# Gate rows of a gated DeltaNet layer read back from HBM, a mask for two heads at once, and one logarithm for queries and keys

## The chip, the cores and the metric

The kernel runs on one core of a Trainium2 chip. The metric is the device time of one execution in microseconds (us); smaller is better. Three runs of the kernel before gave 2562.58, 2562.96 and 2564.0 us, a median of 2562.96 us.

A core has five engines that run side by side, each working through its own queue in order: PE (TensorE, matrix products; its weight loads are listed as PEld), DVE (VectorE, elementwise work), ACT (ScalarE, functions and copies), POOL (GpSimd) and SP (SyncE, which here issues the transfers between HBM and the on-chip memory). An engine waits in its queue until what its next instruction needs is there.

## The reference

The reference is a trunk of two layers over 256 tokens of width 2048, in float32:

```python
for i in range(DEPTH):                       # DEPTH = 2
    h = rms_norm(x, mixer_norm[i])
    x = x + (diff_attention(h, ...) if i % 2 == 0 else gated_deltanet(h, ...))
    x = x + conv_ffn(rms_norm(x, ffn_norm[i]), ...)
```

The change lies in the gated DeltaNet mixer of layer 1. It has 16 heads of queries and keys and 32 value heads, so each query/key head serves two value heads. What matters here of its reference:

```python
q = l2_norm(q.reshape(b, s, 16, 128)); k = l2_norm(k.reshape(b, s, 16, 128))
beta = sigmoid(b_gate)
g = -exp(a_log) * softplus(a_gate + dt_bias)
# per value head and per chunk of 64 tokens
q = q * 128 ** -0.5
g_c = cumsum(g)
decay = exp(where(tril, g_c[:, None] - g_c[None, :], -inf))
low = where(strict, (k * beta) @ k.T * decay, 0)
qk  = where(tril, q @ k.T * decay, 0)
```

The kernel works with two blocks of 128 tokens in place of chunks of 64. For each value head it needs the decay of every token against every other one: the exponential of a running sum along a row, plus a column term per token (the negative running sum and the logarithm of beta), with the later tokens masked out. The running sum of a head is one row of 256 numbers; to stand in the decay table, which has 128 partitions, it must be present in all of them.

## The kernel before, in words

Weights stream from HBM through the core. `weights` (lines 72 to 85) loads a chunk of 512 KB into the tile `raw` (3 buffers, issued by SP, L82), ACT copies it rounded into `whi` (4 buffers, L83), and DVE subtracts to get the rest, `wlo` (4 buffers, L84). `dense` (L95) multiplies a chunk into PSUM: in the DeltaNet layer three products per weight tile (L110, L111, L113); `dense_tok` (L140) does the same with tokens on the partitions (L153 to L155). After every chunk the generators in `bg` advance by one step (`tick`, L67); each `yield` in them puts what follows one chunk later in program order. The framework then writes each engine's queue: it takes instructions in program order as priority, lets one go ahead when its own estimate says that its inputs and a buffer are there, and fills gaps with later ones. The order on an engine is fixed from then on.

`gdn` (L439) runs the mixer. First comes the gate projection, from which `gates` (L732) makes `col` (a column term per token and head, L775) and `rows` (the running sums of all 32 heads as rows, L777 to L782; the rounded value in partitions 0 to 31 and the rest in 32 to 63). Then four blocks of four query/key heads follow. In a block the order of chunks is: the four query/key projections, one value projection, two groups of the output gate `z` (dense_tok), the other value projections; and then, from the second block on, the output projection of the block before (`out`, L687).

For each query/key head `keys` (L485) runs as a generator:

- It squares queries and keys (`sq`, L488), and splits the squares into two parts (`sp`, L489).
- For each of the two value heads POOL spreads a column of the constant `hot` into a 128 x 128 selector (L500), and PE multiplies the selector with `rows` (L502), which puts that head's row into all partitions of a PSUM bank. DVE adds column term and mask, in two instructions per value head (L505), into `d`. 
- PE sums the squares over the partitions (`total`, L241). ACT takes two logarithms, one for the queries and one for the keys (L511 and L512), because the queries' carries the factor 128, then one exponential for both (L513). 
- ACT takes two exponentials per value head (L516 and L517), the second straight from PSUM.
- PE multiplies keys with keys and queries with keys (L525, L526), and DVE multiplies these with `d` into `lt` and `qkt` (L531, L532). POOL copies blocks of `lt` into `Cc` (L536).

`invert` (L540) and `levels` (L565) invert the triangular matrices, and `group` (L618) makes the outputs of two query/key heads; its last step transposes them (L679) for the output projection.

Of the kernel before, what the change touches and what calls it, by code (L numbers as in the profile page):

```python
# [8 lines left out]
F32 = mybir.dt.float32  # L9
# [7 lines left out]
P = 128  # L17
# [8 lines left out]
class Trunk:  # L26
# [8 lines left out]
    def __init__(self, ctx, tc):  # L35
# [402 lines left out]

    def gdn(self, w_gate, w_in, w_z, w_out, nb, hb, gate_ap, const_ap, hot_ap, conv_col, ng, done):  # L439

# [11 lines left out]
        with tc.tile_pool(name="gd", bufs=1) as gd:  # L452
            self.spawn(self.norm_stat())
            con = gd.tile([P, 384], F32, tag="con", name="con")[:, :384]
            nc.sync.dma_start(con, const_ap)
            ident, mask, triu = con[:, :P], con[:, P:T], con[:, T:]
            hot = gd.tile([P, nv], F32, tag="hot", name="hot")
            nc.sync.dma_start(hot, hot_ap)
            gp = gd.tile([P, 2, nv], F32, tag="gp", name="gp")
            nc.sync.dma_start(gp, gate_ap)  # L460
            eps128 = gd.tile([P, 1], F32, tag="eps128", name="eps128")
            nc.vector.memset(eps128, P * EPS)
            TTs, Tas = [], []
# [21 lines left out]
            def keys(hq, c, cc, b0, res):  # L485

                sq = gd.tile([P, 2, T], F32, tag="qs", name="qs", bufs=2)
                nc.scalar.square(sq, c)  # L488
                sp = gd.tile([P, 2, 2, T], F32R, tag="qp", name="qp", bufs=1)  # L489
                self.split(sp, sq)  # L490
                yield
                yield
                while "rows" not in gates:
                    yield
                gb, gc = mp(), gates["col"]
                ds = []
                for v in range(2):
                    h = 2 * hq + v
                    sel = gd.tile([P, P], F32R, tag="sel", name="sel", bufs=2)
                    nc.gpsimd.tensor_copy(sel, hot[:, h:h + 1].to_broadcast([P, P]))  # L500
                    g = gb[:, v * T:(v + 1) * T]
                    nc.tensor.matmul(g, sel, gates["rows"], start=True, stop=True)  # L502
                    d = gd.tile([P, 384], F32, tag="d", name="d", bufs=2)
                    for t in range(2):
                        nc.vector.scalar_tensor_tensor(  # L505
                            d[:, (1 - t) * P:(2 - t) * P], g[:, t * P:(t + 1) * P], gc[:, t, h:h + 1], mask, ALU.add, ALU.add)
                    ds.append(d)
                pn = mp()
                with self.lnexp(self.total(pn, [sp])):
                    pq, pk = self.apart(pn)[:, 0, :], self.apart(pn)[:, 1, :]  # L510
                    nc.scalar.activation(sq[:, 0, :], pq, AF.Ln, bias=eps128, scale=float(P))  # L511
                    nc.scalar.activation(sq[:, 1, :], pk, AF.Ln, bias=self.eps, scale=1.0)  # L512
                    nc.scalar.activation(sq, sq, AF.Exp, scale=-0.5)  # L513
                    for v, d in enumerate(ds):
                        h = 2 * hq + v
                        nc.scalar.activation(d[:, :T], d[:, :T], AF.Exp)  # L516
                        nc.scalar.activation(d[:, T:], gb[:, v * T + P:(v + 1) * T], AF.Exp, bias=gc[:, 0, h:h + 1])  # L517
                nc.vector.tensor_tensor(c, c, sq, ALU.mult)
                q, k = c[:, 0, :], c[:, 1, :]
                yield  # L520
                yield
                prods = []
                for r in (k, q):
                    p = mp()
                    nc.tensor.matmul(p[:, :P], k[:, P:], r[:, P:], start=True, stop=True)  # L525
                    nc.tensor.matmul(p[:, P:384], k[:, :P], r, start=True, stop=True)  # L526
                    prods.append(p)
                for v in range(2):
                    lt = gd.tile([P, 384], F32, tag="lt", name="lt", bufs=2 * hb)
                    qkt = gd.tile([P, 384], F32, tag="qkt", name="qkt", bufs=2 * hb)  # L530
                    nc.vector.tensor_tensor(lt, prods[0][:, :384], ds[v], ALU.mult)  # L531
                    nc.vector.tensor_tensor(qkt, prods[1][:, :384], ds[v], ALU.mult)  # L532
                    b = b0 + v
                    lv = lt[:, :T].rearrange("p (t c) -> p t c", t=2)
# [3 lines left out]
                    res.append((lt, qkt))  # L538

# [78 lines left out]
            def group(gi, gr, lqs, inv, vt, ready, zts, acts):  # L618
# [73 lines left out]
            pg = self.dense(w_gate, KD, self.h_acts, tiles=1, wide=False)  # L692
            self.spawn(self.gates(gd, pg, nv, gp, ident, triu, gates))
            pend = None
# [36 lines left out]

    def gates(self, gd, pg, nv, gp, ident, triu, res):  # L732

        nc, mp = self.nc, self.mp
        t0 = gd.tile([P, 4, 2, 64], F32, tag="vz", name="gt0", bufs=4)
        t1 = gd.tile([P, 4, 2, 64], F32, tag="vz", name="gt1", bufs=4)
# [42 lines left out]
        nc.tensor.matmul(pr[:, P:], w[:, 1, :], triu, start=False, stop=True)  # L779
        rows = gd.tile([P, T], F32R, tag="grow", name="grow")  # L780
        nc.scalar.copy(rows, pr)
# [16 lines left out]
def _layout(inputs):  # L798
# [41 lines left out]
    def turned(w):  # L840
# [18 lines left out]
        "const": np.concatenate(const, 1).astype(f),  # L859
        "hot": np.concatenate([np.eye(NV)] * 2 + [np.zeros((P - 2 * NV, NV))]).astype(f),  # L860
        "w_up1": blocks(x["ffn_w_up"][1], KD, up),
# [5 lines left out]
def trunk_kernel(tc, a, out):  # L867
    nc = tc.nc
    with ExitStack() as ctx:
# [30 lines left out]
        def start(k):  # L900

            if len(begun) <= k:
# [11 lines left out]
        t.ffn(a["w_up0"], a["w_down0"], NJ, a["fcols0"], then(mixer, 1))  # L914
        t.gdn(a["w_gate"], a["w_in"], a["w_z"], a["w_out"], NB, HB, a["gate"], a["const"], a["hot"],
              lambda tap, tile_: one(gconv, tap * 4 * NQ + tile_), ng, then(ffn, 1))
# [17 lines left out]
```

## Time and profile before

| what | value |
|---|---|
| median of three runs | 2562.96 us |
| the profiled execution | 2563.51 us |
| its span, first to last instruction | 2561.7 us |
| mean granted clock of TensorE | 0.998 |
| PE busy | 2541.3 us |
| DVE busy | 1910.1 us |
| ACT busy | 1503.9 us |
| POOL busy | 107.1 us |
| DeltaNet mixer | about 1063 to 1885 us of the span |

The profiled execution is 0.55 us above the median, and 1.8 us of it lie outside the span. "Busy" of PE counts a product from its start to its modelled end; products are pipelined, so that one may start about 0.11 us after another and still be listed with 0.28 us. What a product costs is read from the distance between starts.

### The profile page before, as it was taken

Reading aid. Unit: us, or ns where it says so; the run is one execution under the profiler, and the core shown is the slowest. Engines: PE = TensorE matmul, PEld = TensorE weight load, DVE = VectorE, ACT = ScalarE, POOL = GpSimd, SP = SyncE. Lnnn points to the kernel's source line nnn. Section 1 sums busy time; section 2 is a strip of 40 time slices with the busy share of each in tenths; the row PEclk is TensorE's granted clock in tenths of the full one; section 3 lists DMA queues with packets and bytes.
Section 4 is the critical chain, followed back from the end, with each engine's and each line's share of the span. In section 5 each row is a group of like instructions: output and inputs, shape, how many; then the busy total and the mean of one; then the engine's idle time right before and its main releaser. Section 6 shows DMA issues by size and latency. Waiting matters only on the chain.

```text
span 2561.7 us, 44240 instructions
## 1 busy us (share of the span) xinstructions
PE 2541.3 (99%) x17456; PEld 2366.3 (92%) x17456; DVE 1910.1 (75%) x2846; ACT 1503.9 (59%) x2094; POOL 107.1 (4%) x221
## 2 busy tenths in 40 slices
PE   8999999999999999999999999999999999999999
PEld 7998899999999999999989999999999999999998
DVE  7876677777878655689789688689687778786554
ACT  6666656666666444585674674674566666665433
POOL 0000000000000000010121021021000000000000
PEclk9999999999999999999999999999999999999999
DMA  6555566665666666656455455455466666666665
GB/s 216 184 178 174 173 199 202 202 201 202 201 201 203 199 203 200 193 166 198 141 161 194 133 177 182 138 167 188 148 200 201 202 201 202 200 200 207 207 209 162
DMA packets 135425, 481.02 MB, mean 188 GB/s; under 512 B 15409, under 2 KB 18481, under 8 KB 135217
## 3 DMA queue, kind: packets, MB, share of 16 engines
q1 hardware_dynamic: 134064, 475.58, 57.8%
q8 instruction: 137, 2.24, 0.3%
q10 hardware_dynamic: 1152, 2.61, 0.3%
q14 instruction: 72, 0.58, 0.1%
HBM read 476.03 MB, written 2.10 MB: 187 GB/s over the span
## 4 chain that ended last, share of the span: by engine, by line
PE 94%; DVE 2%; ACT 2%; issue 1%; DMA 1%; POOL 0%; SPq 0%; ACTq 0%; DVEq 0%
PE ps L110 47%; PE ps L111 27%; PE ps L113 6%; PE ps L153 3%; PE ps L154 3%; PE ps L155 3%; PE mp L635 2%; DVE wlo L84 1%; PE mp L241 1%; ACT whi L83 1%; DMA raw<-w_in 0%; PE mp L526 0%; PE mp L605 0%; PE mp L600 0%; DMA raw<-w_qk 0%
## 5 line engine op out<-in xcount | busy, mean ns | idle before, releaser
L84 DVE TENSOR_TENSOR wlo<-raw,whi 128x1024 fp32r<-128x1024 f32 (+2 forms) x909 | 1104.5, 1216 | 546.9 <-ACT whi L83 538.7
L83 ACT CAST whi<-raw 128x1024 fp32r<-128x1024 f32 (+2 forms) x909 | 944.4, 1040 | 853.7 <-PE ps L110 597.3
L110 PE MATMUL ps<-h,whi 128*128 128x512 f32 (+1 forms) x4304 | 1363.4, 358 | 9.6 <-DVE h L168 6.0
L111 PE MATMUL ps<-h,wlo 128*128 128x256 f32 x4304 | 1181.0, 274 | 1.5 <-DVE wlo L84 1.5
L110 PEld LDWEIGHTS ps<-h,whi 128*128 128x128 f32 x4304 | 818.9, 190 | 96.8 <-DVE h L168 6.0
L111 PEld LDWEIGHTS ps<-h,wlo 128*128 128x128 f32 x4304 | 828.5, 193 | 3.6 <-DVE wlo L84 2.3
L110 PE MATMUL ps<-ac,whi 128*128 128x512 f32 x1632 | 535.0, 382 | 0.0
L111 PE MATMUL ps<-ac,wlo 128*128 128x256 f32 x1632 | 444.7, 273 | 0.0
L110 PEld LDWEIGHTS ps<-ac,whi 128*128 128x128 f32 x1632 | 308.4, 189 | 42.9 <-PE ps L110 0.2
L111 PEld LDWEIGHTS ps<-ac,wlo 128*128 128x128 f32 x1632 | 313.3, 192 | 0.1
L113 PE MATMUL ps<-h,whi 128*128 128x256 f32 x1040 | 287.3, 276 | 0.0
L113 PEld LDWEIGHTS ps<-h,whi 128*128 128x128 f32 x1040 | 200.3, 193 | 0.4
L154 PE MATMUL ps<-wlo,h 128*128 128x512 f32 x384 | 146.2, 381 | 0.0
L155 PE MATMUL ps<-whi,h 128*128 128x512 f32 x384 | 145.9, 380 | 0.0
L153 PE MATMUL ps<-whi,h 128*128 128x512 f32 x384 | 145.8, 380 | 0.0
L222 DVE SCALAR_TENSOR_TENSOR cv<-u,fcols,cv 128x255 f32<-128x255 f32 (+1 forms) x344 | 142.8, 477 | 0.0
L111 PE MATMUL ps<-oc,wlo 128*128 128x256 f32 x512 | 141.9, 277 | 0.0
L110 PE MATMUL ps<-oc,whi 128*128 128x256 f32 x512 | 141.7, 277 | 0.0
L113 PE MATMUL ps<-oc,whi 128*128 128x256 f32 x512 | 141.4, 277 | 0.0
L111 PEld LDWEIGHTS ps<-oc,wlo 128*128 128x128 f32 x512 | 98.3, 192 | 0.2
L110 PEld LDWEIGHTS ps<-oc,whi 128*128 128x128 f32 x512 | 98.3, 192 | 0.2
L113 PEld LDWEIGHTS ps<-oc,whi 128*128 128x128 f32 x512 | 98.2, 192 | 0.1
(201 smaller groups left out, 2108.5 us busy)
## 6 DMA issues: line engine op xcount, KB each, us to landing
raw<-w_up SPq DMA_DIRECT2D x344, 512.0 KB, 4.7
raw<-w_down SPq DMA_DIRECT2D x160, 512.0 KB, 3.7
raw<-w_in SPq DMA_DIRECT2D x128, 512.0 KB, 4.5
raw<-w_z SPq DMA_DIRECT2D x64, 512.0 KB, 3.6
raw<-w_out SPq DMA_DIRECT2D x64, 512.0 KB, 4.4
raw<-w_qk SPq DMA_DIRECT2D x63, 512.0 KB, 4.5
raw<-w_v SPq DMA_DIRECT2D x32, 512.0 KB, 3.5
raw<-w_o SPq DMA_DIRECT2D x32, 512.0 KB, 4.5
```

The lines of the kernel that those rows point to most:

```text
L83: nc.scalar.copy(hi, raw)
L84: nc.vector.tensor_tensor(lo, raw, hi.bitcast(F32), ALU.subtract)
L110: nc.tensor.matmul(ps[:, c, :n], hi[:, k, s], self.turns(a[:, :n // T, :]), start=first, stop=False)
L111: nc.tensor.matmul(ps[:, c, :T], lo[:, k, s], self.turns(a[:, :1, :]), start=False, stop=last and wide)
L113: nc.tensor.matmul(ps[:, c, :T], hi[:, k, s], self.turns(a[:, 1:, :]), start=False, stop=last)
L153: nc.tensor.matmul(ps[:, c, :], ah, wh, start=first, stop=False)
L154: nc.tensor.matmul(ps[:, c, :], ah, wl, start=False, stop=False)
L155: nc.tensor.matmul(ps[:, c, :], al, wh, start=False, stop=last)
L222: nc.vector.scalar_tensor_tensor(out[:, j:], u[:, :T - j], taps[n - 1 - j], out[:, j:], ALU.mult, ALU.add)
L241: last = self.nc.tensor.matmul(out, self.onesr, self.pairs(p[:, j]), start=i + j == 0, stop=i + j == n)
L635: nc.tensor.matmul(p[:, v, :], l(v), r[:, v, :], start=i == 0, stop=i == len(terms) - 1)
```

## The change

The running sums of the 32 heads are laid out as 32 rows of 384 numbers: the second block of 128 tokens, then both blocks. They are written to a buffer in HBM once. For each query/key head a transfer then reads two rows of it (one for each value head) and puts them into all 128 partitions of a tile `d` of 128 x 2 x 384. That takes the place of the selectors, the selector products and the constant `hot`. The mask is added to both value heads in one DVE instruction; the column term moves into the bias of the exponentials. One logarithm serves queries and keys, and the queries' factor moves into the product that makes `qkt`. The tiles `lt`, `qkt` and `d` hold both value heads; `d` has still two buffers, so that it now holds two query/key heads. The triangle `triu` and the rows before their transfer lie in a buffer of the tag `qs`, which the squares use too. The second set of rows in partitions 32 to 63 is gone. `group` yields once more ahead of its transposes.

```diff
+        self.dr = ctx.enter_context(tc.tile_pool(name="dr", bufs=1, space=bass.MemoryType.DRAM))
...
-            con = gd.tile([P, 384], F32, tag="con", name="con")[:, :384]
-            nc.sync.dma_start(con, const_ap)
-            ident, mask, triu = con[:, :P], con[:, P:T], con[:, T:]
-            hot = gd.tile([P, nv], F32, tag="hot", name="hot")
-            nc.sync.dma_start(hot, hot_ap)
+            con = gd.tile([P, T], F32, tag="con", name="con")
+            nc.sync.dma_start(con, const_ap[:, :T])
+            ident, mask = con[:, :P], con[:, P:]
+            early = gd.tile([P, 2 * T], F32, tag="qs", name="early", bufs=2)
+            nc.sync.dma_start(early[:, :P], const_ap[:, T:])
...
-                gb, gc = mp(), gates["col"]
-                ds = []
-                for v in range(2):
-                    h = 2 * hq + v
-                    sel = gd.tile([P, P], F32R, tag="sel", name="sel", bufs=2)
-                    nc.gpsimd.tensor_copy(sel, hot[:, h:h + 1].to_broadcast([P, P]))
-                    g = gb[:, v * T:(v + 1) * T]
-                    nc.tensor.matmul(g, sel, gates["rows"], start=True, stop=True)
-                    d = gd.tile([P, 384], F32, tag="d", name="d", bufs=2)
-                    for t in range(2):
-                        nc.vector.scalar_tensor_tensor(
-                            d[:, (1 - t) * P:(2 - t) * P], g[:, t * P:(t + 1) * P], gc[:, t, h:h + 1], mask, ALU.add, ALU.add)
-                    ds.append(d)
+                gc = gates["col"]
+                d = gd.tile([P, 2, 384], F32, tag="d", name="d", bufs=2)
+                nc.sync.dma_start(d, gates["rows"][2 * hq:2 * hq + 2, :].unsqueeze(0).to_broadcast([P, 2, 384]))
+                dv = d[:, :, :T].rearrange("p v (t c) -> p v t c", t=2)
+                m4 = mask.unsqueeze(1).unsqueeze(1).to_broadcast([P, 2, 2, P])
+                nc.vector.tensor_tensor(dv, dv, m4, ALU.add)
                 pn = mp()
                 with self.lnexp(self.total(pn, [sp])):
-                    pq, pk = self.apart(pn)[:, 0, :], self.apart(pn)[:, 1, :]
-                    nc.scalar.activation(sq[:, 0, :], pq, AF.Ln, bias=eps128, scale=float(P))
-                    nc.scalar.activation(sq[:, 1, :], pk, AF.Ln, bias=self.eps, scale=1.0)
-                    nc.scalar.activation(sq, sq, AF.Exp, scale=-0.5)
-                    for v, d in enumerate(ds):
-                        h = 2 * hq + v
-                        nc.scalar.activation(d[:, :T], d[:, :T], AF.Exp)
-                        nc.scalar.activation(d[:, T:], gb[:, v * T + P:(v + 1) * T], AF.Exp, bias=gc[:, 0, h:h + 1])
+                    self.rsqrt(sq, self.apart(pn), 1)
+                    for v in range(2):
+                        for t, s in ((1, d[:, v, :P]), (0, d[:, v, P:])):
+                            nc.scalar.activation(s, s, AF.Exp, bias=gc[:, t, 2 * hq + v:2 * hq + v + 1])
...
+                lt = gd.tile([P, 2, 384], F32, tag="lt", name="lt", bufs=hb)
+                qkt = gd.tile([P, 2, 384], F32, tag="qkt", name="qkt", bufs=hb)
                 for v in range(2):
-                    lt = gd.tile([P, 384], F32, tag="lt", name="lt", bufs=2 * hb)
-                    qkt = gd.tile([P, 384], F32, tag="qkt", name="qkt", bufs=2 * hb)
-                    nc.vector.tensor_tensor(lt, prods[0][:, :384], ds[v], ALU.mult)
-                    nc.vector.tensor_tensor(qkt, prods[1][:, :384], ds[v], ALU.mult)
+                    nc.vector.tensor_tensor(lt[:, v], prods[0][:, :384], d[:, v], ALU.mult)
+                    nc.vector.scalar_tensor_tensor(
+                        qkt[:, v], prods[1][:, :384], P ** -0.5, d[:, v], ALU.mult, ALU.mult)
+                for v in range(2):
...
                     ys.append(y)
                 yield
                 yield
+                yield
                 for v0 in range(0, n, 2):
...
-            for d in range(2):
-                nc.vector.scalar_tensor_tensor(
-                    w[:, t, 32 * d:32 * d + nv], q[:, t, nv:], -1.0, a, ALU.mult, ALU.mult)
+            nc.vector.scalar_tensor_tensor(w[:, t, :nv], q[:, t, nv:], -1.0, a, ALU.mult, ALU.mult)
...
-        rows = gd.tile([P, T], F32R, tag="grow", name="grow")
-        nc.scalar.copy(rows, pr)
-        nc.vector.tensor_tensor(rows[32:64], pr[32:64], rows[32:64].bitcast(F32), ALU.subtract)
-        res["rows"], res["col"] = rows, col
+        nc.scalar.copy(rows[:, P:], pr[:nv])
+        nc.scalar.copy(rows[:, :P], pr[:nv, P:])
+        res["rows"] = self.dr.tile([nv, 384], F32, tag="grow", name="grow")
+        nc.sync.dma_start(res["rows"], rows)
+        res["col"] = col
```

In `gates`, `triu` and `rows` are now `early[:, :P]` and `early[:nv, P:]`.

More of the change, by code (lines that the diff above doesn't have):

```diff
@@ L437, in await_, with gdn @@
         return items[k]
-    def gdn(self, w_gate, w_in, w_z, w_out, nb, hb, gate_ap, const_ap, hot_ap, conv_col, ng, done):
+    def gdn(self, w_gate, w_in, w_z, w_out, nb, hb, gate_ap, const_ap, conv_col, ng, done):
         nc, tc, mp = self.nc, self.tc, self.mp
@@ L527, in keys @@
                     prods.append(p)
+                lt = gd.tile([P, 2, 384], F32, tag="lt", name="lt", bufs=hb)
+                qkt = gd.tile([P, 2, 384], F32, tag="qkt", name="qkt", bufs=hb)
                 for v in range(2):
-                    lt = gd.tile([P, 384], F32, tag="lt", name="lt", bufs=2 * hb)
-                    qkt = gd.tile([P, 384], F32, tag="qkt", name="qkt", bufs=2 * hb)
-                    nc.vector.tensor_tensor(lt, prods[0][:, :384], ds[v], ALU.mult)
-                    nc.vector.tensor_tensor(qkt, prods[1][:, :384], ds[v], ALU.mult)
+                    nc.vector.tensor_tensor(lt[:, v], prods[0][:, :384], d[:, v], ALU.mult)
+                    nc.vector.scalar_tensor_tensor(
+                        qkt[:, v], prods[1][:, :384], P ** -0.5, d[:, v], ALU.mult, ALU.mult)
+                for v in range(2):
                     b = b0 + v
-                    lv = lt[:, :T].rearrange("p (t c) -> p t c", t=2)
+                    lv = lt[:, v, :T].rearrange("p (t c) -> p t c", t=2)
                     for r in quad:
@@ L537, in keys @@
                             cc[r, :, 2 * b:2 * b + 2].rearrange("p c t -> p t c"), lv[r, :, r])
-                    res.append((lt, qkt))
+                    res.append((lt[:, v], qkt[:, v]))
             def invert(cc, lqs, inv):
@@ L692, in gdn @@
             pg = self.dense(w_gate, KD, self.h_acts, tiles=1, wide=False)
-            self.spawn(self.gates(gd, pg, nv, gp, ident, triu, gates))
+            self.spawn(self.gates(gd, pg, nv, gp, ident, early, gates))
             pend = None
@@ L730, in gdn, with gates @@
             out(*pend)
-    def gates(self, gd, pg, nv, gp, ident, triu, res):
+    def gates(self, gd, pg, nv, gp, ident, early, res):
         nc, mp = self.nc, self.mp
+        triu, rows = early[:, :P], early[:nv, P:]
         t0 = gd.tile([P, 4, 2, 64], F32, tag="vz", name="gt0", bufs=4)
@@ L859, in _layout @@
         "const": np.concatenate(const, 1).astype(f),
-        "hot": np.concatenate([np.eye(NV)] * 2 + [np.zeros((P - 2 * NV, NV))]).astype(f),
         "w_up1": blocks(x["ffn_w_up"][1], KD, up),
@@ L914, in trunk_kernel @@
         t.ffn(a["w_up0"], a["w_down0"], NJ, a["fcols0"], then(mixer, 1))
-        t.gdn(a["w_gate"], a["w_in"], a["w_z"], a["w_out"], NB, HB, a["gate"], a["const"], a["hot"],
+        t.gdn(a["w_gate"], a["w_in"], a["w_z"], a["w_out"], NB, HB, a["gate"], a["const"],
               lambda tap, tile_: one(gconv, tap * 4 * NQ + tile_), ng, then(ffn, 1))
```

2 lines of the change are left out of this document (removed).

## The prediction

> **What bounds the kernel now.** The page comes first: the span, the busy shares, and the chain that ended last.
>
> ```profile
> span 2561.7 us, 44240 instructions
> ...
> PE 2541.3 (99%) x17456; PEld 2366.3 (92%) x17456; DVE 1910.1 (75%) x2846; ACT 1503.9 (59%) x2094; POOL 107.1 (4%) x221
> ...
> PE 94%; DVE 2%; ACT 2%; issue 1%; DMA 1%; POOL 0%; SPq 0%; ACTq 0%; DVEq 0%
> ```
>
> PE is busy for 99% and carries 94% of the chain, so at first order the time is what PE has to stream. Work taken from PE counts in full; work taken from DVE, ACT, POOL or the queue of transfers counts only where PE waits for it. Next come the stage that the change touches and one crowded stretch of it, in the table by stretches (columns: length, busy time of PE, weight loads, DVE, ACT and POOL, granted clock, share of the DMA engines, GB/s).
>
> ```profile
> 1063.00:1885.00 822.00, 817.26 (x7076) 786.93 (x7075) 669.66 (x1143) 510.97 (x715) 106.94 (x217) 1.00 0.52 168
> ...
> 1140.00:1160.00 20.00, 20.00 (x101) 17.68 (x100) 15.75 (x24) 17.34 (x25) 7.27 (x15) 1.00 0.61 185
> ```
>
> PE is idle for 822.0 - 817.3 = 4.7 us of the mixer at the full granted clock. DVE (81%) and ACT (62%) have room on average, but ACT has little where the heads are prepared: 17.3 of 20 us. The DMA engines have 48% free. The waits of PE in this stage, one row for each cause (total, times, longest):
>
> ```profile
> PE mp L744 <- DVE glin L133: 1.7, 1, 1.7
> PE mp L581 <- DVE tcc L562: 1.5, 1, 1.5
> PE mp L241 <- ACT qp L233: 0.9, 2, 0.7
> PE mp L502 <- DVE lt L531: 0.6, 1, 0.6
> ```
>
> They are all that a lighter DVE or ACT could give back: 4.7 us together, of which only the last belongs to an instruction that is removed.
>
> **Selector products: 3.8 us off PE.** There are 32 of them (16 heads by two). What one costs shows in the distance between starts on the timeline of PE:
>
> ```profile
> 1114.49 0.28 PE L113 MATMUL ps<-h,whi 128*128 128x256 f32 x1
> 1114.60 0.28 PE L502 MATMUL mp<-grow,sel 128*128 128x256 f32 x1
> 1114.72 0.27 PE L110 MATMUL ps<-h,whi 128*128 128x256 f32 x1
> ...
> 1285.13 0.28 PE L110 MATMUL ps<-h,whi 128*128 128x256 f32 x1
> 1286.01 0.36 PE L502 MATMUL mp<-grow,sel 128*128 128x256 f32 x1 [0.61 <-DVE lt L531]
> ```
>
> The product ahead of it has 0.11 us, the selector product 0.12 us. So 32 x 0.12 = 3.8 us, at the least 32 x 0.11 = 3.5 us. The group's row below says 11.3 us; that sums overlapping durations, and it would be the upper end only if nothing were pipelined, which the starts exclude. Some selector products start behind products of full float32 and stand longer in the trace; I take that as a price of the change of type, which the next product then pays, and count no gain for it. The second place is the one where PE waited 0.6 us for the selector product, whose PSUM bank was still being read by L531. With the product, the wait goes, and a PSUM bank per head is asked for less: -0.6 us (ends 0 and -0.9, if the next product L241 finds nothing to wait for either). No weight load is saved in time: they run beside the products.
>
> **DVE, ACT and POOL: lighter, at no gain in the sum.** The groups that change (busy time, mean ns of one, idle before):
>
> ```profile
> L500 POOL CAST sel<-hot 128x128 fp32r<-128x128 f32 x32 | 18.9, 592 | 288.1 <-PE mp L502 286.9 <-DMA hot<-hot 0.5
> L502 PE MATMUL mp<-grow,sel 128*128 128x256 f32 x32 | 11.3, 353 | 0.6 <-DVE lt L531 0.6
> L505 DVE SCALAR_TENSOR_TENSOR d<-mp,gc,con 128x128 f32<-128x128 f32 x64 | 19.2, 340 | 0.5 <-PE mp L502 0.5
> L511 ACT ACTIVATE qs<-mp,eps 128x256 f32<-128x256 f32 x16 | 7.6, 475 | 0.2
> L512 ACT ACTIVATE qs<-mp,eps 128x256 f32<-128x256 f32 x16 | 7.5, 468 | 0.0
> L517 ACT ACT_TABLE_LOAD x6 | 7.7, 1283 | 0.1
> L518 DVE TENSOR_TENSOR cv<-cv,qs 128x512 f32<-128x512 f32 x16 | 10.9, 684 | 0.0
> ...
> L228 ACT ACTIVATE ri<-mp,eps 128x512 f32<-128x512 f32 x16 | 11.0, 688 | 11.0 <-PE mp L241 11.0
> ```
>
> DVE loses 64 additions (19.2 us) and gains 16 of 128 x 512, which I price like L518 (10.9 us): -8.3 us, 0.5 us a head. ACT trades L511 and L512 for one logarithm of 128 x 512 as in L228: 7.6 + 7.5 - 11.0 = -4.1 us, 0.26 us a head. The exponentials stay two of 128 and two of 256 columns a head. The six table loads at L517 (7.7 us) exist because another function came between the logarithms and these exponentials; some may go. POOL loses 18.9 us. `qkt` stays one instruction for one. PE waits for none of this beyond the rows above, so the sum has 0; the end below is the whole of the other waits, -(1.7 + 1.5 + 0.9) = -4.1 us. The end above is 0, since nothing here grows.
>
> **Transfers: 0 in the sum, covered by the buffered weights.** Each head now asks for 128 x 2 x 384 x 4 B = 384 KB on the queue that carries the weights. SP issues 17 transfers more in all (16 reads and the write; `hot` goes, `early` comes). What the trace shows of transfers (size, median us to landing; the page's row has the share of 16 engines over the span):
>
> ```profile
> q1 hardware_dynamic: 134064, 475.58, 57.8%
> ...
> raw<-w_in SPq DMA_DIRECT2D x128, 512.0 KB, 4.5
> ...
> out<-x SPq DMA_DIRECT2D x16, 128.0 KB, 3.3
> ...
> POOL sel L500 <- PE mp L502: 286.9, 20, 72.2
> ...
> SPq L82 <- DVE wlo L84: 1511.5, 626, 6.5
> ```
>
> The engines move 475.58 MB in 0.578 x 2561.7 = 1481 us, or 393 kB in 1.2 us. That is the least by which a read holds up the weights queued behind it; the most is a whole landing of 4.5 us, as if nothing overlapped. A read of one HBM row by all partitions occurs nowhere in this trace; I take 1.2 us, as raw<-w_in is nearest in size, and keep 4.5 us for the range. A read is asked for as soon as a buffer of `d` is free: the selectors show that the planner hoists so, as POOL stood up to 72 us in front of a selector's buffer. SP itself has the time: it waits 1511 us for DVE to free `raw`. With two buffers the read for head n follows L532 of head n - 2, one head's projection before its use (4 chunks of 24 products, 4 x 24 x 0.11 = 10.6 us). The new wait stands on DVE: the mask addition waits for its landing, and the next `wlo` is queued behind it, for which PE's L111 or L154 waits. What covers both delays is how far the split weights run ahead of PE. I counted that for each of the 260 chunks of the mixer (end of the chunk's L84 to its first product with `wlo`); it is mostly 4 to 7 us, and least at the first group of `z`:
>
> ```profile
> 1140.19 1.21 DVE L84 TENSOR_TENSOR wlo<-raw,whi 128x1024 fp32r<-128x1024 f32 x1
> ```
> ```profile
> 1143.34 0.38 PE L154 MATMUL ps<-wlo,h 128*128 128x512 f32 x1
> ```
>
> Here the split ends at 1141.4 and PE first uses it at 1143.3: 1.9 us. This stretch comes once in each of the four blocks. A delay of 1.2 us fits in it; were the cover gone, each read would cost PE its 1.2 us, 16 x 1.2 = 19 us.
>
> One page of the Trainium skill speaks against the change: "DMA: Bandwidth & Descriptors", in "Latency and other measured facts", tells of per-partition streams that run in step at an unlucky row pitch and fall from 207 to 103 GB/s, and infers that they meet on the same HBM channels. Streams that all read one row might meet likewise. By that rule the hold-up would be twice 1.2 us, 2.4 us, the four thinnest places would give way by 0.5 us each, and the sum would rise by 2 us to -2.4 us; no run so far shows which it is.
>
> **The write, once.** Before, the rows were ready on chip; now two copies, a write and a read stand in their place ahead of the first head.
>
> ```profile
> 1107.30 0.35 ACT L781 CAST grow<-mp 128x256 fp32r<-128x256 f32 x1
> ```
> ```profile
> L505 DVE SCALAR_TENSOR_TENSOR d<-mp,gc,con x64: 332/340/352, 1111.9 to 1704.6; 128x128 f32<-128x128 f32 x64
> ...
> L531 DVE TENSOR_TENSOR lt<-mp,d x32: 540/548/558, 1121.5 to 1712.9; 128x384 f32<-128x384 f32 x32
> ```
>
> Two copies of 0.35 us end at 1108.0; a write like out<-x (3.3 us) lands at 1111.3, a read (4.5 us) at 1115.8. The mask was at 1111.9, so it comes 4 us later; addition and exponentials need about 2.3 us, and the product L531 was at 1121.5. So it is hidden: 0. SP waits for the copies and then for the write, with the next weights behind it; the ends are 0 and +4 us, should neither the three `raw` buffers nor the four of the split weights cover it. The second head's squares wait for the same write, as `early` holds one of the two `qs` buffers; it lies in the same shadow.
>
> **The further yield** ranks the transposes L679 one chunk later. The waits of PE hold no row for L679, and the output projection of a block comes at least a block of chunks later, or, for the last block, behind the 16 chunks of the block before. 0; if that cover failed, one chunk of 24 products, 24 x 0.11 = 2.7 us.
>
> **Sum.** -3.8 - 0.6 = -4.4 us. Against the profiled execution's 2563.5 us that is 2559.1 us; that execution lies 0.55 us above the median of the runs, so I predict 2562.96 - 4.4 = 2558.6 us, or -0.17%. About 0.2%, or 5.1 us, is what a measurement of this kernel can tell from no change.
>
> **Rivals.** *Faster by more:* with DVE and ACT lighter and PSUM less contended, the three other waits go too: -4.4 - 4.1 = -8.5, 2554.5 us. For it speaks that two of them follow on DVE or ACT work of this very stage; against it, that the order of each engine is drawn up anew from estimates, so waits of this kind will appear elsewhere. *Slower: the weights behind a read come late.* If a read holds them up by a full landing of 4.5 us, the thinnest place of each block loses 4.5 - 1.9 = 2.6 us: 4 x 2.6 = 10.4, less 4.4, gives 2569.0 us. It decides for slower by 0.2% from (5.1 + 4.4) / 4 + 1.9 = 4.3 us per read on; below 1.9 us it costs nothing. For it: ACT is nearly full in that stretch, so a late chunk is not soon made good. Against it: the DMA engines have 39% free there. *The change does not do what it says:* PE gets its products later in other places and fills the 4.4 us with new waits, so 2563.0 us. Against it: the weights run 4 us and more ahead nearly everywhere.
>
> **How the numbers follow.** I give the forecast 0.50, with its own range from 2556.5 to 2561 us (0.12 of the 0.50 lies beyond the bound at 2557.8 us, towards faster), faster by more 0.22, the late weights 0.20, no effect 0.08. So faster 0.12 + 0.22 = 0.34, the same 0.38 + 0.08 = 0.46, slower 0.20. The range goes from 2554 us, the faster rival with a half us to spare, to 2569 us, the slower one.
>
> **What would show it.** Right: L502, L500 and `hot` are gone; PE has 32 products fewer, its busy time in the mixer falls by about 4 us; the reads of `d` land within about 5 us, and DVE's waits for them are short; PE's waits in the mixer stay at 4 to 5 us. Wrong: a row of PE waiting for `wlo` or `whi` in the first group of `z`, ACT waiting longer for raw<-w_in or raw<-w_z (the late weights); a wait of DVE for `d` of several us a head; PE waiting for L679's or L682's results (the yield); or waits in the mixer that add up to 9 us, which would eat the gain.

## The result and the profile after

The changed kernel takes 2567.99 us (median of 22 runs, 2562.22 to 2574.19), the kernel before 2562.92 us beside it (22 runs, 2560.24 to 2566.52). The ratio is 1.0020 with a 95% interval from 1.0014 to 1.0026: 5 us slower, where 4.4 us faster was forecast. The time lies in the stated range, but it moved the other way, by about as much as the prediction held to be the least that can be told from no change. The profiled execution took 2569.32 us.

The page of the changed kernel, the lines that answer to those of before:

```profile
span 2567.5 us, 44044 instructions
...
PE 2539.0 (99%) x17424; PEld 2362.1 (92%) x17424; DVE 1900.4 (74%) x2794; ACT 1501.8 (58%) x2076; POOL 88.6 (3%) x189
...
q1 hardware_dynamic: 136416, 481.91, 58.6%
...
PE 85%; DVE 6%; DMA 4%; ACT 3%; issue 2%; SPq 0%; ACTq 0%; DVEq 0%
```

Every engine has less to do: PE 32 products and 2.3 us, DVE 9.7 us, ACT 2.1 us, POOL 18.5 us. Yet the span is 5.8 us longer, and the chain that ended last is now PE for 85% in place of 94%; DVE has gone from 2% to 6% and transfers from 1% to 4%. So the time is waiting. The waits of PE in the mixer (window 1063 to 1890 us of the span; total, times, longest):

```profile
PE ps L111 <- ACT zt L705: 2.9, 1, 2.9
PE mp L571 <- DVE tcc L552: 2.7, 2, 1.6
PE ps L155 <- DVE wlo L85: 1.8, 1, 1.8
PE mp L513 <- DVE cv L506: 1.8, 2, 1.5
PE mp L736 <- DVE glin L134: 1.7, 1, 1.7
PE mp L670 <- DVE zt L659: 0.7, 1, 0.7
PE mp L242 <- ACT qp L234: 0.4, 1, 0.4
```

They add up to 12.0 us, against 4.7 us before. (Line numbers are one higher than before in the first part of the code and some ten lower behind the head's work: L85 is the split, L83 its load, L496 the read of `d`, L499 the mask addition.) The waits of the other engines in the same window, and of SP over the whole span:

```profile
ACT whi L84 <- DMA raw<-w_in: 47.7, 32, 4.4
DVE d L499 <- DMA d<-grow: 27.1, 15, 4.4
ACT whi L84 <- DMA raw<-w_z: 22.2, 11, 5.0
```
```profile
SPq L496 <- DVE qkt L520: 24.1, 14, 2.7
```

DVE waits for the landing at 15 of the 16 mask additions, 27.1 us in all. ACT's waits for the weights w_in and w_z, 22.5 + 11.8 us before, have doubled; the mask addition on POOL, below, has them nearly as long (45.5 + 20.7 us) and loses nothing. And SP stands 24.1 us in front of reads, until DVE has finished with the buffer of `d`. The reads themselves (size, median us to landing) are in no way slow:

```profile
raw<-w_in SPq DMA_DIRECT2D x128, 512.0 KB, 4.4
...
d<-grow SPq DMA_DIRECT2D x16, 384.0 KB, 4.1
```

One of these waits, followed on three engines. The timeline of DVE in the first block:

```profile
1133.76 1.01 DVE L520 SCALAR_TENSOR_TENSOR qkt<-mp,d 128x384 f32<-128x384 f32 x2
1134.69 0.68 DVE L134 TENSOR_TENSOR u<-ps,rstd 128x512 f32<-128x512 f32 x1
1139.21 0.69 DVE L499 TENSOR_TENSOR d<-d,con 128x512 f32<-128x512 f32 x1 [3.85 <-DMA d<-grow]
1139.82 1.22 DVE L85 TENSOR_TENSOR wlo<-raw,whi 128x1024 fp32r<-128x1024 f32 x1
```

That of SP, and of PE:

```profile
1132.15 0.33 SPq L83 DMA_DIRECT2D raw<-w_z  x1
1134.80 0.33 SPq L496 DMA_DIRECT2D d<-grow  x1
1141.06 0.33 SPq L83 DMA_DIRECT2D raw<-w_z  x1
```
```profile
1138.88 0.38 PE L154 MATMUL ps<-whi,h 128*128 128x512 f32 x1
1141.09 0.48 PE L155 MATMUL ps<-wlo,h 128*128 128x512 f32 x1 [1.83 <-DVE wlo L85]
```

`qkt` frees a buffer of `d` at 1134.8, and SP asks for the next read at once. But the mask addition that needs this read is the second instruction behind `qkt` on DVE. DVE comes to it at 1135.4 and stands until 1139.2. The split of the next weights is behind it; it ends at 1141.0, and PE, which had run out of split weights, goes on at 1141.1. The split also frees `raw`, so SP can ask for further weights only at 1141.1, 8.9 us after the last ones, and ACT waits 2.2 us for these at 1144.6. That second delay shows in no row of PE.

A second wait of PE hangs on a read without any weights in between. DVE stands 2.24 us for the read, the scaling of queries and keys (`cv`, L506) is three instructions behind, and PE waits 1.54 us for it:

```profile
1125.24 0.69 DVE L499 TENSOR_TENSOR d<-d,con 128x512 f32<-128x512 f32 x1 [2.24 <-DMA d<-grow]
...
1127.59 0.68 DVE L506 TENSOR_TENSOR cv<-cv,qs 128x512 f32<-128x512 f32 x1
```
```profile
1128.42 0.46 PE L513 MATMUL mp<-cv 128*128 128x128 f32 x2 [1.54 <-DVE cv L506]
```

### The profile page after: what moved, and what is told of

It is laid out like the page before. It is cut to its first block, busy times and chain, and to the rows that moved or that the text cites. A ratio compares the mean times of both kernels' runs of the same rounds, so it can differ in the third digit from the quotient of the medians.

```text
span 2567.5 us, 44044 instructions
## 1 busy us (share of the span) xinstructions
PE 2539.0 (99%) x17424; PEld 2362.1 (92%) x17424; DVE 1900.4 (74%) x2794; ACT 1501.8 (58%) x2076; POOL 88.6 (3%) x189
## 3 DMA queue, kind: packets, MB, share of 16 engines
q1 hardware_dynamic: 136416, 481.91, 58.6%
q8 instruction: 137, 2.24, 0.4%
## 4 chain that ended last, share of the span: by engine, by line
PE 85%; DVE 6%; DMA 4%; ACT 3%; issue 2%; SPq 0%; ACTq 0%; DVEq 0%
PE ps L111 46%; PE ps L112 25%; PE ps L114 4%; DVE wlo L85 3%; PE mp L625 2%; PE ps L154 2%; PE ps L156 2%; PE ps L155 2%; DMA raw<-w_in 1%; DMA d<-grow 1%; ACT whi L84 1%; DMA raw<-w_z 1%; DVE cv L223 1%; PE mp L242 0%; DVE tmp L543 0%
## 5 line engine op out<-in xcount | busy, mean ns | idle before, releaser
L85 DVE TENSOR_TENSOR wlo<-raw,whi 128x1024 fp32r<-128x1024 f32 (+2 forms) x909 | 1103.7, 1215 | 531.5 <-ACT whi L84 522.8
L156 PE MATMUL ps<-whi,h 128*128 128x512 f32 x384 | 146.0, 380 | 0.0
```

The costliest lines, as they stand in the source:

```text
L85: nc.vector.tensor_tensor(lo, raw, hi.bitcast(F32), ALU.subtract)
L156: nc.tensor.matmul(ps[:, c, :], al, wh, start=False, stop=last)
```

## The experiments

Three theories were set against each other. A: DVE stands in its queue at the mask addition until the read has landed, and the splits behind it come late. B: SP stands in front of a read, and the weights queued behind it come late. C: each engine's order was drawn up anew, and the waits are chance, or those of added work, not the read's. Each ratio is against runs of the kernel before on the same chip; the medians of before were 2562.92 us for the first four runs below, 2562.24 or 2562.38 us for those behind them, and 2563.75 us for the last ones, in which the gate functions are forced ahead. Where the text says how far the orders of two kernels agree, the instructions of an engine were taken from both traces by operation and tiles and set side by side.

**The mask addition on POOL.**

```diff
-                nc.vector.tensor_tensor(dv, dv, m4, ALU.add)
+                nc.gpsimd.tensor_tensor(dv, dv, m4, ALU.add)
```

> The changed kernel with the mask addition issued on POOL in place of DVE; reads of d, their queue and everything else as in the change. Theory A (DVE stands in its queue at the mask addition until the read has landed, 27.1 us in 15 waits, and the split of the weights behind it comes late): DVE's wait for d<-grow is gone, PE's waits in the mixer fall from 11 to about 5 us, and the time falls from 2568 to 2559-2561 us. Theory B (SP stands in front of a read until DVE has freed d, 24.1 us in 14 waits, and the weights queued behind the read come late): nothing of that is changed, so 2566-2569 us, with PE's waits still near 11 us. Theory C (every engine's order was drawn up anew, and the waits are chance, not the read's): no reason for a fall of more than 3 us.

Measured: 2559.96 us, ratio 0.9988 (0.9979 to 0.9997), 8 us under the change and a little under the kernel before. POOL now does the waiting (window 1063 to 1890 us), and SP stands for `d` as long as it did:

```profile
POOL d L499 <- DMA d<-grow: 72.2, 11, 46.3
```
```profile
SPq L496 <- DVE qkt L520: 25.7, 14, 3.3
```

PE's waits in the mixer are down to 4.1 us:

```profile
PE mp L736 <- DVE glin L134: 1.4, 1, 1.4
PE mp L571 <- DVE tcc L552: 1.0, 2, 0.8
PE ps L112 <- DVE wlo L85: 0.9, 1, 0.9
PE mp L513 <- DVE cv L506: 0.8, 1, 0.8
```

The addition itself is slower there (mean 1704 ns against 692 on DVE), which nothing waits for. The queue, the reads and SP's wait are those of the change, so B is out as the main cause. C isn't out by this run, as the order was drawn anew with the edit: about 140 of DVE's other 2778 instructions stand elsewhere.

**No reads.**

```diff
-                nc.sync.dma_start(d, gates["rows"][2 * hq:2 * hq + 2, :].unsqueeze(0).to_broadcast([P, 2, 384]))
+                nc.gpsimd.memset(d, -1e30)
```

> The changed kernel without the 16 reads: d is filled by a POOL memset instead, so the decay table is not computed from the gate rows. All other instructions stay. It shows what the change is worth without its transfers. Theories A and B: 2558-2560 us (the -4.4 us of the prediction's sum), DVE waits for d at most 1 us a head. Theory C: stays within 2 us of 2568.

Measured: 2560.32 us, ratio 0.9988 (0.9979 to 0.9997). This is what the change is worth without its transfers: 2.6 us, and the reads cost 2568.0 - 2560.3 = 7.7 us. The two were measured apart, each beside a kernel before of 2562.92 us; their intervals leave some 3 us either way (an estimate).

This pair says the most, since its order hardly differs: all but 15 of DVE's 2794 instructions, 8 of ACT's 2076 and 19 of PE's 17424 come in the same order in both. So the 7.7 us aren't those of a redrawn order. PE's waits in the mixer are 5.8 us here and 12.0 in the change. The waits that go are all for results of DVE: the split (1.8 us), `cv` (1.8) and `tcc` (2.7). `tcc` belongs to the inversion, 57 and 60 us behind the last mask addition before it, and it goes with the reads; by what way they bring it about is argued, not shown. For a lag carried along speaks that DVE is behind up to there: between 1172 and 1214 us in the change a split ends 1.7 us ahead of its first product (median), and 4.9 us ahead without the reads.

DVE still waits here, for the memset, 13.9 us in 9 waits, more than the 1 us a head that was expected, but none over 2.1 us: that much is covered. PE's longest wait in the mixer of the change, 2.9 us for `zt`, is nearly all there without any read:

```profile
PE ps L111 <- ACT zt L705: 2.4, 1, 2.4
```

**Reads that nobody uses, in the kernel before.**

```diff
-                    nc.vector.tensor_tensor(qkt, prods[1][:, :384], ds[v], ALU.mult)
+                    m = nc.vector.tensor_tensor(qkt, prods[1][:, :384], ds[v], ALU.mult)
...
                     res.append((lt, qkt))
+                dd = gd.tile([P, 2, P], F32, tag="dd", name="dd", bufs=1)
+                rd = nc.sync.dma_start(dd, const_ap[2 * hq:2 * hq + 2, :P].unsqueeze(0).to_broadcast([P, 2, P]))
+                self.tc.add_manual_dep(rd.ins, m.ins.name, DATA)
```

> The kernel before, with one read a head added that nobody uses: two rows of a constant into all partitions, 128 KB (no room for 384 KB), asked for on the weights' queue once the head's qkt is made, as in the change. Theory A: no DVE instruction waits for it, so 2563 us within 1.5 us. Theory B: SP stands for qkt with the weights behind, so most of the loss shows: 2566-2569 us.

Measured: 2562.83 us, ratio 0.9998 (0.9989 to 1.0007). SP stands 19.4 us for `qkt` in front of these reads, with the weights behind, and it costs nothing; PE, DVE and ACT run exactly the order of the kernel before. The reads are a third of the real ones in size, so this speaks against SP's standing, not on the bytes.

**The same reads, with a mask addition on DVE that waits for them.** Added to the kernel of the run above:

```diff
+                nc.vector.tensor_tensor(dd, dd, mask.unsqueeze(1).to_broadcast([P, 2, P]), ALU.add)
```

> As the kernel with unused reads, and a mask addition on DVE (128 x 256) that waits for each of them; the selector products stay. Theory A: DVE waits for dd some 1.5 us in most of the 16 cases, PE's waits in the mixer rise by 4-8 us, 2566-2572 us. Theory B: the same time as with unused reads within 1.5 us, and 0.4 us a head of DVE work more, hidden.

Measured: 2568.69 us, ratio 1.0021 (1.0012 to 1.0030), with DVE waiting 16.9 us in 14 waits. That is what A asks for, but it needs its control.

**The control: the same addition with no read.** In the kernel of the run above:

```diff
-                rd = nc.sync.dma_start(dd, const_ap[2 * hq:2 * hq + 2, :P].unsqueeze(0).to_broadcast([P, 2, P]))
+                rd = nc.gpsimd.memset(dd, 0.0)
```

> The control for the masked reads: the kernel before with the same DVE addition (128 x 256) once a head, but its tile is filled by a POOL memset, with no read. It has the added DVE work (16 x 0.4 us) and a newly drawn order, not the landing. Theory A: 2563 us within 1.5 us. Theory C (added work and the new order made the loss): 2567-2570 us, like the masked reads.

Measured: 2569.69 us, ratio 1.0028 (1.0018 to 1.0038); a single further run of the same kernel gave 2568.38 us. So here the expectation of A failed: an addition of 0.4 us a head, without a read, costs 7 us in the kernel before, and the masked reads alone prove nothing on landing. Beside the control they show a limit of A: their orders are nearly the same (32 of DVE's 2862 instructions differ), DVE waits 16.9 us in the one and 6.5 us in the other, and the one that waits more isn't slower. Waits of DVE of up to 2.4 us cost nothing there; in the change they reach 4.4 us. The control's waits of PE (window 1063 to 1895 us) name other places:

```profile
PE mp L683 <- DVE zt L673: 3.7, 2, 3.4
PE ps L110 <- ACT zt L718: 2.8, 1, 2.8
```

The second of them stands in the changed kernel too (L705). The timeline of ACT in the second block of the control, and then of the kernel before, shows what it is:

```profile
1335.28 1.28 ACT L718 ACT_TABLE_LOAD   x1
1336.58 2.42 ACT L718 ACTIVATE zt<-ps,rstd 128x512 f32<-128x512 f32 x4
```
```profile
1330.68 1.27 ACT L714 ACTIVATE zt<-ps,rstd 128x512 f32<-128x512 f32 x2
...
1336.57 1.28 ACT L714 ACTIVATE zt<-ps,rstd 128x512 f32<-128x512 f32 x2 [1.49 <-PE ps L155]
```

The gate functions free the two PSUM banks of the `z` groups. Before, those of the first group run 6 us ahead of the second's; in the control all four come together behind the second group's products, and PE finds no bank. So C holds in part, for this kernel: a small addition can draw the order anew for the worse (some 230 of DVE's 2846 instructions stand elsewhere than before).

**The mask addition on DVE, held back.**

```diff
-                nc.vector.tensor_tensor(dv, dv, m4, ALU.add)
                 pn = mp()
-                with self.lnexp(self.total(pn, [sp])):
+                tot = self.total(pn, [sp])
+                m = nc.vector.tensor_tensor(dv, dv, m4, ALU.add)
+                self.tc.add_manual_dep(m.ins, tot.ins.name, DATA)
+                with self.lnexp(tot):
```

> The changed kernel with one dependency more: the mask addition, still on DVE, may go into DVE's order only behind the head's sum of squares on PE (L242). The read is asked for as before and has longer to land. Theory A: DVE's wait for the reads falls from 27 us to under 8 us, PE's waits in the mixer to 5-7 us, 2559-2563 us. Theory B: 2566-2569 us, since SP's wait and the queue stay.

Measured: 2562.02 us, ratio 0.9998 (0.9989 to 1.0007). The addition is still on DVE and the reads are the same; its place in DVE's order is later, though 164 of DVE's 2794 instructions stand elsewhere, not its 16 alone. Its wait has all but gone, while SP's is longer than in the change (window 1063 to 1890 us, and the whole span):

```profile
DVE d L501 <- DMA d<-grow: 1.4, 1, 1.4
```
```profile
SPq L496 <- DVE qkt L522: 30.8, 14, 4.1
```

**The reads issued by POOL.**

```diff
-                nc.sync.dma_start(d, gates["rows"][2 * hq:2 * hq + 2, :].unsqueeze(0).to_broadcast([P, 2, 384]))
+                nc.gpsimd.dma_start(d, gates["rows"][2 * hq:2 * hq + 2, :].unsqueeze(0).to_broadcast([P, 2, 384]))
```

> The changed kernel with the 16 reads issued by POOL in place of SP; the mask addition stays on DVE. SP no longer stands in front of a read. Theory A (DVE waits for the landing): DVE still waits for d, 20 us or more in all, and the time stays at 2566-2572 us. Theory B (SP stands for d, and the weights queue behind): the loss goes, 2559-2562 us.

Measured: 2578.49 us, ratio 1.0053 (1.0041 to 1.0066). SP stands in front of no read any more, and it gets worse, beyond what either theory gave: the reads land later (median 4.5 us), and DVE waits more:

```profile
DVE d L499 <- DMA d<-grow: 36.7, 13, 5.6
```

The order is nearly that of the change (70 of DVE's instructions and 90 of PE's differ). So in nearly one order DVE's waits of 13.9, 27.1 and 36.7 us (no reads, the change, this run) go with 2560.3, 2568.0 and 2578.5 us. Not all of the last step is waiting: PE's waits in the mixer are 18.1 us in place of 12.0, and the granted clock falls to 0.50 for 3.4 us at five places of the mixer, each just behind a wait of PE, in place of one in the change.

**Without the further yield**, with the mask on DVE and on POOL:

```diff
                 yield
                 yield
-                yield
                 for v0 in range(0, n, 2):
```

> The changed kernel without the further yield ahead of the transposes. The prediction gave the yield no cost: 2568 us within 2 us. If the yield made part of the loss (the transposes late, the longest wait of PE, 2.9 us, at a matter of the output gate): 2563-2566 us. The order is drawn anew, so single waits will move.

> The changed kernel with the mask addition on POOL and without the further yield. With the mask on DVE the missing yield cost 6 us. Theory A: that was DVE's wait again (32.6 us there, longest 6.8), so without it 2559-2562 us, as with the yield. Theory C, in the form that the yield itself carries the gain: 2565-2568 us.

Measured: 2574.29 us (ratio 1.0040, 1.0027 to 1.0052) with the mask on DVE, 2560.40 us (0.9990, 0.9981 to 0.9998) with it on POOL. So the yield is worth 6 us where DVE waits and nothing that can be told where it doesn't, though the orders were drawn anew in both pairs. In the first of the two DVE waits longer still, and PE 5.3 us for `zt`:

```profile
DVE d L499 <- DMA d<-grow: 32.6, 14, 6.8
...
PE ps L111 <- ACT zt L704: 5.3, 1, 5.3
```

**The further yield alone, and with the control.** The line `yield` added to the kernel before, and to the control.

> The kernel before with the further yield alone. The prediction gave it nothing: 2562.5 us within 1.5 us. In the kernel before PE has no wait at the transposes that it could take away; what moves is the drawn order.

> The kernel before with the added DVE addition (no read) and the further yield ahead of the transposes. Without the yield this took 2569.7 us, with PE waiting 3.7 us for the transposes' input and 2.8 us for a bank that ACT frees late. If the place of the transposes in PE's order is what cost it: 2562-2565 us, and the wait for zt at the transposes falls under 1 us. If the added DVE work itself costs: 2568-2571 us.

Measured: 2561.18 us alone (ratio 0.9995, 0.9986 to 1.0003): nothing that can be told. With the control 2570.55 us (1.0032, 1.0020 to 1.0044): PE's wait at the transposes is gone, and the time is not; the wait for `zt` is 3.3 us now, and smaller ones have come.

**One logarithm alone, in the kernel before.**

```diff
-                    pq, pk = self.apart(pn)[:, 0, :], self.apart(pn)[:, 1, :]
-                    nc.scalar.activation(sq[:, 0, :], pq, AF.Ln, bias=eps128, scale=float(P))
-                    nc.scalar.activation(sq[:, 1, :], pk, AF.Ln, bias=self.eps, scale=1.0)
-                    nc.scalar.activation(sq, sq, AF.Exp, scale=-0.5)
+                    self.rsqrt(sq, self.apart(pn), 1)
...
-                    nc.vector.tensor_tensor(qkt, prods[1][:, :384], ds[v], ALU.mult)
+                    nc.vector.scalar_tensor_tensor(
+                        qkt, prods[1][:, :384], P ** -0.5, ds[v], ALU.mult, ALU.mult)
```

> The kernel before with the one logarithm alone (and the queries' factor in the product that makes qkt). The prediction gave it no gain, since ACT loses 0.26 us a head beside PE: 2563 us within 1.5 us; if ACT's relief lets PE's other waits go, 2559-2561 us.

Measured: 2560.29 us, ratio 0.9992 (0.9983 to 1.0001). It may be worth 2 us; the interval just reaches no change.

**The gate functions forced ahead.** In the changed kernel, the control and the kernel with the mask on POOL, the fifth chunk of the second `z` group is split only behind the first group's gate functions:

```diff
-        nc.scalar.copy(hi, raw)
+        h = nc.scalar.copy(hi, raw)
+        if behind is not None:
+            self.tc.add_manual_dep(h.ins, behind.ins.name, DATA)
...
```

> The changed kernel, with one dependency more: the split of the fifth weight chunk of the second z group may go into ACT's order only behind the gate functions of the first z group, which free the first group's PSUM bank. If two causes share the loss (A: DVE's wait for the reads; D: in block 1 ACT's order puts the gate functions of both z groups behind the second group's products, so that PE finds no free bank, 2.9 us): PE's wait for zt goes, DVE's wait for d stays near 27 us, 2564-2566 us. If A alone made the loss: 2567-2569 us, with PE's wait turning up elsewhere.

> The control with the same dependency: the kernel before, an added DVE addition without a read, the gate functions of the first z group ahead of the fifth chunk of the second. D: PE's wait for zt (2.8 us) goes, 2565-2567 us in place of 2569.7. If the added DVE work costs in other ways: 2569-2571 us.

> The changed kernel with the mask on POOL and the same dependency. With the mask on POOL the first group's gate functions already came early enough (13 us after the second group's start), so the dependency has nothing to give: 2560 us within 1.5 us.

Measured: 2584.28 us (ratio 1.0081, 1.0067 to 1.0094), 2572.95 us and 2571.48 us (both 1.0033, 1.0020 to 1.0045). All three are slower than without the dependency, the last by 11 us where nothing was expected to happen. PE waits for `zt` no more; it waits for the split that now stands behind it (L156), and in the changed kernel still longer for results of DVE:

```profile
PE mp L515 <- DVE cv L508: 8.1, 3, 5.0
PE ps L157 <- DVE wlo L87: 6.0, 5, 1.6
PE ps L156 <- ACT whi L84: 4.3, 1, 4.3
```

The edit moved the wait and added to it, so it doesn't tell the two causes apart. What does is the run without reads: it has nearly the order of the change, its late gate functions too, and not the 7.7 us.

## Why the prediction was wrong

**Selector products and PE's wait for their bank: right in kind, smaller in net.** 32 products went, and with them the wait of 0.6 us. Four versions in which DVE hardly stands for the reads come to 2560.0, 2560.3, 2560.4 and 2562.0 us, 0.2 to 3.0 us under the kernel before, for the 4.4 us of the sum. In the run without reads the rest fits the 2.4 us for `zt`; in the others it isn't placed. A fifth, with the mask on POOL and the gate functions forced ahead, takes 2571.5 us for waits of its own.

**The step that failed: the mask addition's wait, which the prediction covered with "A delay of 1.2 us fits in it".** Two things were run together there. The hold-up of the weights behind a read was priced at 1.2 us of transfer time, and that was near enough (below). The wait of DVE for the read was named, but given no price of its own: it was taken to be covered, as the read would be asked for a head's projection, 10.6 us, before its use. That interval counts to the exponentials. The mask addition needs only the read, and the planner, which the prediction itself had seen hoist the selectors, hoisted it as well, to the second place behind `qkt` in the timeline shown. DVE then stands for nearly the whole landing there: 3.85 us in a place for which the split weights had had 1.9 us to spare, and PE waits 1.83 us. The term was a wait of up to 4.4 us on DVE, in 15 places and 27.1 us in all, not a delay of 1.2 us, and with it the reads cost 7.7 us of the kernel's time. Leaving out the reads ends the loss in nearly the same order. That it is DVE's place, and not the reads themselves, is shown by the addition on POOL and the addition held back: both end it with the reads left as they are, though in a redrawn order. The prediction also named only `wlo` as what is queued behind the addition; `cv` was as costly in PE's rows.

The cover itself was read a little too high. Counted in the trace of the kernel before, the least is not 1.9 us: a split leads by 1.6 us at 1501 us, and by 0.9 us at 1725 us, behind the last head. Of the prediction's own signs of being wrong, DVE's waits for `d` and PE's waits in the mixer (12.0 us, against the 9 named) came true as costs; ACT's longer waits for the weights came too, and were harmless.

**The slower rival: the right time by the wrong way.** It gave 2569.0 us for weights that come late behind a read in the queue; 2568.0 us came out. But unused reads in that queue cost nothing, SP's standing of 23 to 31 us is harmless in three versions of 2560.0 to 2562.0 us, and taking the reads off SP's queue made it worse. That the number is so near is luck.

**The read of one row by all partitions.** The 16 reads landed in 4.1 us (median; 3.2 to 5.2). The share of the engines went from 57.8% of 2561.7 us to 58.6% of 2567.5 us, 1481 to 1505 us, which is some 1.5 us a read for the 1.2 us assumed. The prediction's estimate from the figures on row pitch in the Trainium skill ("DMA: Bandwidth & Descriptors", "Latency and other measured facts") was 2.4 us: the halving that the page gives for unlucky pitches doesn't carry over to these reads of one row by all partitions.

**The write, once.** Hidden, as predicted. The read for the first head was asked for at 1111.1 us and its addition began at 1115.2, where 1115.8 had been worked out.

**DVE, ACT and POOL.** DVE lost 9.7 us for 8.3 predicted, POOL 18.5 for 18.9. ACT's busy time fell by 2.1 for 4.1, but that figure counts instructions that overlap once; their durations added up fell by 4.0 us. The logarithm gave 4.1 as predicted, and two terms that the prediction didn't have cancel. The exponentials did not stay what they were: the wide ones have a column of biases now and take 496 ns (414 before), the narrow ones, which had it already, read `d` in place of PSUM and take 390 ns (362 before).

```profile
L505 ACT ACTIVATE d<-d,gc 128x256 f32<-128x256 f32 x32 | 15.9, 496 | 0.0
L505 ACT ACTIVATE d<-d,gc 128x128 f32<-128x128 f32 x32 | 12.5, 390 | 0.0
```

That is 32 x 82 + 32 x 28 ns = 3.5 us more, where the prediction said that nothing grows. Three fewer table loads in all (3.8 us) make up for it. No gain in time was forecast from this, and the one logarithm alone shows none that its interval makes certain.

**The further yield.** Nothing by itself, as predicted. In the changed kernel it saves 6 us, which the prediction didn't see.

**What stays open.** Why an addition of 0.4 us a head on DVE, without a read, costs the kernel before 7 us. The trace shows where PE waits (the gate functions together at the end of the second `z` group, the last transposes), and that removing one of these waits brings others; what makes the planner draw that order wasn't settled. So part of what separates most of these kernels is the order drawn, by amounts as large as the effect of the change. The statement on the reads rests on the runs that keep the order, those without reads and with the reads issued by POOL, and on the three versions with reads of full size in which DVE hardly waits. How the 7.7 us divide between the split, `cv` and the later lag of DVE is known only as far as PE's waits show it.

## What to carry to other kernels

Where a planner or a program order moves a transfer forward, it can move the first instruction that uses it along, as it did here; an instruction that waits for a transfer belongs on an engine that has nothing else to do, or behind something that comes late enough. Price a new wait by its landing time and by what is queued behind it on its engine: here waits of up to 4.4 us on DVE held up split weights and the inputs of PE's next products, while 72 us on POOL cost nothing. A saving of 4 us on the engine that bounds the kernel is smaller than what a redrawn order can take, so before a cause is named, compare several versions, and see in the traces how far the orders of a pair agree: a pair in one order says more than one with a faster time.

## What the runs showed of the hardware

A read of two rows of 1.5 KB each from HBM into all 128 partitions (384 KB) lands in 4.1 us, between the 3.3 us of a like read of 128 KB and the 4.4 us of 512 KB of plain weights. Issued by POOL in place of SP it landed in 4.5 us. The addition of 128 x 512 numbers takes 1.70 us on POOL and 0.69 us on DVE. In the profiled execution of the change the granted clock is 0.50 for 3.4 us from 1341.9 us, as PE's wait of 2.9 us ends.
